# A gated unit turned and made from seven block products, with every engine's order laid out word by word

## The chip, the cores and the metric

One core of one Trainium2 chip runs the kernel. Its engines are TensorE (PE: matmuls, its weight loads shown as PEld), VectorE (DVE), ScalarE (ACT) and GpSimd (POOL); SyncE (SP) and POOL issue the transfers. The metric is the device time of one launch in microseconds, and the number to compare is the median of several runs. Inputs and outputs are float32 in the chip's memory. A matmul of full precision is made from halves: a float32 number is split into a high part, which the matmul form `fp32r` can hold, and a low part, and `high x high + high x low + low x high` makes three matmuls for one.

## The reference

With DEPTH = 1 there is one layer. Its mixer is the bidirectional S5 scan with a gated linear unit behind it, and its feed-forward part is a SwiGLU. There are 1024 tokens with 1024 features, 256 context tokens, and a hidden width of 2816 (22 tiles of 128). What matters here, shortened:

```python
def rms_norm(x, g):
    y = x * rsqrt(mean(x * x, -1, keepdims=True) + 1e-6)
    return y * g

# mixer, behind the scan that gives y (1024 tokens x 1024 features)
y = y + d_skip * h
g = gelu(y)
m = g * sigmoid(g @ w_glu + b_glu)          # the gated unit
x = x + gate0 * m                           # adaLN gate, residual
# feed-forward
h2 = rms_norm(x, norm_ffn) * (1 + scale1) + shift1
x = x + gate1 * ((silu(h2 @ w1) * (h2 @ w3)) @ w2)
return rms_norm(x, norm_final)
```

gate0, scale1, shift1 and gate1 are rows of 1024 features that the conditioning vector c gives.

## The kernel before

The kernel is one program with an order written by hand. Memory on the chip is cut into fixed regions (`r0`, `ra`, `ru`, `c0` to `c3`, `rxa`, `rxc`, `rw`), and code places views in them; PSUM comes from pools. The framework sets a wait wherever a buffer's last use isn't done, and each engine runs its own instructions in the order in which the code issued them.

The scan's part is driven by two strings of words, `PROG1` and `PROG2`, which `run()` carries out one after the other: a letter for the operation and a number for its index. In the trace the scan's recurrence on DVE ends at about 229 us. `PROG2` then finishes the scan's outputs block by block (k is a block of 128 features, of 8): words N, Q, Z and D make and add up the parts of block k, H applies GELU to it (ACT, from PSUM into the array `Y`, 128 partitions holding 128 token groups, 8 feature blocks x 8 token sets s x 128), I turns four of its 128x128 squares by transposes (`gt_hi`, L1056) and makes the high half, J the low half, w, l, W and V load and split weights, x multiplies Y by gate0 on POOL, and g starts the first matmuls.

The gated unit is then made with the activations as the stationary side. For token set s (128 tokens) and column quarter cq (256 outputs), `glu_unit(cq, s)` issues 8 x 3 matmuls of 128x256 (`glu_mm`, L1097 to L1099), adds the bias row on DVE (L77), applies the sigmoid on ACT (L1127), multiplies by gated g and adds x on DVE, and squares with a sum for the norm on ACT (L1134). There are 32 such units; first 16 for the first half of the tokens, then 16 for the second half. Between them generators run: `rms_steps` (L1157) makes the norm's factor on DVE, `h2s_steps` scales rows of Y on POOL, and `h2t_steps` transposes them back (L1177), applies scale and shift on ACT (L1186) or DVE (L86), and splits them (L1188 and L77). So `GH[0]` and `GH[1]` hold h2, turned, for the two token halves.

The first two FFN tiles follow plainly: `up_plain(ft, n)` makes 4 x 12 matmuls of 128x512 (`mm4` and `mm3`, L1286 to L1288) for token half n. `load2(0)`, behind `up_plain(0, 0)`, gates the first tile of w2 (`gate2`, 128x1024 on DVE) and splits it (cast on ACT, low half on POOL). The other twenty tiles are done two by two from seven products of blocks (`seq`, `produce`), which the change leaves as they are.

Names that recur: `tt` is a two-input elementwise instruction, and all its calls carry the helper's line L77 (L78 after the change), whatever engine they run on; `stt` is L80, `ts` L84 or L86. `split` makes both halves: a cast (ACT, by `S.copy`) and the subtraction of it (POOL or DVE). `MB` is a gate spread over the partitions, `mcol` the modulation rows as columns, `ident` the identity for transposes. In the profile's names, `pe`, `pu`, `pd`, `ut`, `xt`, `pt` are PSUM, and the rest are regions or small tiles (`r`).

Of the kernel before, what the change touches and what calls it, by code (L numbers as in the profile page):

```python
# [10 lines left out]
F32 = mybir.dt.float32  # L11
# [6 lines left out]
P = 128  # L18
# [13 lines left out]
PROG1 = ("A22 B0 A26 C02 G1 A30 A34 C03 A40 K0 A44 A48 C10 K1 L2 A54 G2 C11 A60 F10 C12 F11 C13 T0 T1 T2 T3 A64 M0 M1 K2 R0 P0 Y0 Y1 K3 L3 R1 C20 P1 Y2 Y3 T4 T5 G3 T6 T7 C21 C22 C23 K4 R2 P2 Y4 Y5 K5 R3 P3 Y6 Y7 T8 T9 T10 T11 C30 C31 R4 P4 Y8 Y9 C32 C33 R5 P5 Y10 Y11 M2 m0 F30 F31")  # L32
PROG2 = ("k6 Z0 N0 Z1 Z2 D0 Z3 N1 k7 D1 Z4 H0 H1 K6 N2 D2 H2 K7 T12 T13 T14 T15 N3 Z5 D3 H3 N4 D4 z6 z7 I0 J0 I1 J1 w0 w1 l1 H4 N5 D5 I2 J2 H5 I3 J3 W0 W1 x0 x1 x2 x3"
         " Q6 H6 I4 J4 Q7 b0 I5 J5 H7 g03 g13 I6 J6 g23 g05 g15 I7 J7 V1 w20 w21 g26 x10 x11 x12 x13")
# [8 lines left out]
def s5_ffn_kernel(tc, a, out):  # L43
# [3 lines left out]
    with ctx:  # L47
# [17 lines left out]
        RA = region("ra", 80.5)  # L65
# [3 lines left out]
        RW = region("rw", 6)  # L69

# [33 lines left out]
        modb = small([6, T])[:, 0:2]  # L104
# [49 lines left out]
        xr = a["x"].rearrange("(c s) d -> c s d", s=T)  # L154
# [799 lines left out]
        def run(prog):  # L954


            for w in prog.split():
# [40 lines left out]
                elif op == "N":  # L998
                    late[i] = [pe8([4, T, HC]) for _ in range(2)]
                    states_mm(i, late[i], 1, HSl[i], True)  # L1000
                elif op == "D":
                    for gp, po in enumerate(late[i]):
                        tt(yview(i, gp), po, yview(i, gp), ADD)
                elif op == "H":
                    if i in late:
                        S.activation(Y[:, i], Y[:, i], AF.Gelu_apprx_tanh)
                    else:
                        for gp in range(2):
                            S.activation(yview(i, gp), inner[i][gp], AF.Gelu_apprx_tanh)
                elif op == "I":  # L1010
                    if GH[0] is None:
                        GH[0] = tuple(view(region(t, 16, R32), 0, [4, 8, P]) for t in ("c1", "c0"))
                    late[i] = gt_hi(i, 0)
                elif op == "J":
                    gt_lo(i, 0, late[i])
                elif op == "W":
                    if not WR:
                        W0.append(region("c2", 16, R32))
                        WR.append((view(W0[0], 0, [8 * 256]), view(W0[0], 8, [8 * 256])))
                    v = slice(1024 * i, 1024 * i + 1024)  # L1020
                    split(wr0[i], (WR[0][0][:, v], WR[0][1][:, v]), E, V)
                elif op == "w":
                    cq, h = divmod(i, 10)
                    SY.dma_start(wr0[h], a["w_glu"][cq][:, 1024 * h:1024 * h + 1024])
                elif op == "b":
                    SY.dma_start(bglu, a["b_glu"].to_broadcast([P, D]))
                elif op == "l":
                    load_glu(i)
                elif op == "m":
                    mod_row(0)  # L1030
                elif op == "x":
                    gate(i % 10, slice(4 * (i // 10), 4 * (i // 10) + 4))
                elif op == "V":
                    GR.append(region("ra", 80.5, R32))
                    GH[1] = (view(GR[0], 0, [4, 8, P]), view(GR[0], 16, [4, 8, P]))
                    WR.extend((view(GR[0], kb, [8 * 256]), view(GR[0], kb + 8, [8 * 256])) for kb in (32, 48, 64))
                    split(wraw, WR[i], E)
                elif op == "g":
                    glu_mm(0, i // 10, range(i % 10 + 1))

        KT = {}
        late, W0, WR, PZ, GH, GR = {}, [], [], {}, [None, None], []
        wr0 = [view(RXa, 4, [1024]), view(RW, 0, [1024])]
        bglu = view(RU, 32, [D])
        wraw = view(RXc, 0, [2048])

        def load_glu(cq):
            SY.dma_start(wraw, a["w_glu"][cq])
# [4 lines left out]
        def gt_hi(k, half, eng=S):  # L1053
            pt = pe8([4, P])
            for i in range(4):
                PE.transpose(pt[:, i], Y[:, k, 4 * half + i], ident)  # L1056
            if eng is S:
                S.copy(GH[half][0][:, :, k], pt)
            else:
                eng.tensor_copy(GH[half][0][:, :, k], pt)  # L1060
            return pt

        def gt_lo(k, half, pt):
            h_, l_ = GH[half]
            tt(l_[:, :, k], pt, h_[:, :, k].bitcast(F32), SUB)

        def gt(k, half):
            gt_lo(k, half, gt_hi(k, half))

# [8 lines left out]
        def gh_(s):  # L1078
            h_, l_ = GH[s // 4]
            return h_[:, s % 4], l_[:, s % 4]  # L1080

        def gate(s, ks):
            y = Y[:, ks, s]
            n = y.shape[2] if len(y.shape) == 4 else 0
            g = MB.rearrange("p (k n) -> p k n", n=P)[:, ks]
            tt(y, y, bc(g, 2, n) if n else g, MUL, E)

        def glu_mm(cq, s, ks):

            wH, wL = (w.rearrange("p (k n) -> p k n", k=8) for w in WR[cq])  # L1090
            h_, l_ = gh_(s)
            new = (cq, s) not in PZ
            if new:
                PZ[cq, s] = [pe8([256]), 0]
            pz, n = PZ[cq, s]
            for k in ks[n:]:
                PE.matmul(pz, h_[:, k], wH[:, k], start=n == 0, stop=False)  # L1097
                PE.matmul(pz, h_[:, k], wL[:, k], start=False, stop=False)
                PE.matmul(pz, l_[:, k], wH[:, k], start=False, stop=n == 7)  # L1099
                n += 1  # L1100
            PZ[cq, s][1] = n
            return pz

# [7 lines left out]
        W0, GR = W0[0], GR[0]  # L1111
        X1 = region("c3", 16)
        xs = [view(X1, 4 * i, [D]) for i in range(4)]
        for s in range(4):
            SY.dma_start(xs[s], xr[:, s])
        TT = [[view(GR, 32 + 16 * i + 8 * j, [4, 4, P]) for j in range(2)] for i in range(3)]
        def glu_unit(cq, s, *others):

            def step():
                for g in others:  # L1120
                    next(g, None)

# [650 lines left out]
```

## Time and profile before

| what | us |
|---|---|
| runs shown | 1021.4, 1022.26, 1024.85 |
| median of them | 1022.26 |
| the profiled execution itself | 1024.33 |
| its span, first to last instruction | 1022.5 |
| mean clock granted to TensorE (share of full) | 0.987 |

All rows of the profile are of that one execution, 2.07 us above the median. In a row of a timeline stand start, duration, engine, line and operation, output and inputs (`out<-in`), shapes and count, and in brackets the idle time ahead of it with what ended it. In a row of groups stand the count behind the x, then busy time, the mean duration in nanoseconds, and the engine's idle time ahead of such instructions. Matmuls are pipelined, so that durations of neighbours overlap.

The chain of work that ended last is followed back by the profile to about 1000 us only, over DVE and ACT, which make the last norm and the outputs. The change doesn't touch that part, so the time ahead of it is read from PE's rows.

### The profile page before, as it was taken

Reading aid. Unit: us, or ns where it says so; the run is one execution under the profiler, and the core shown is the slowest. Engines: PE = TensorE matmul, PEld = TensorE weight load, DVE = VectorE, ACT = ScalarE, POOL = GpSimd, SP = SyncE. Lnnn points to the kernel's source line nnn. Section 1 sums busy time; section 2 is a strip of 40 time slices with the busy share of each in tenths; the row PEclk is TensorE's granted clock in tenths of the full one; section 3 lists DMA queues with packets and bytes.
Section 4 is the critical chain, followed back from the end, with each engine's and each line's share of the span. In section 5 each row is a group of like instructions: output and inputs, shape, how many; then the busy total and the mean of one; then the engine's idle time right before and its main releaser. Section 6 shows DMA issues by size and latency. Waiting matters only on the chain. (4 is left out here: it accounts for less than half of the span.)

```text
span 1022.5 us, 18552 instructions
## 1 busy us (share of the span) xinstructions
PE 962.6 (94%) x6988; PEld 774.2 (76%) x6988; DVE 785.6 (77%) x1642; ACT 438.5 (43%) x858; POOL 762.7 (75%) x590
## 2 busy tenths in 40 slices
PE   5987798868999999999999999999999999999996
PEld 1466523658999988778888888888888888888885
DVE  7989799994365778788968768585958778686977
ACT  5477622324353663533334343424333343324337
POOL 5799999991591457879686877778686877777664
PEclk9999999998999999999999999999999999999998
DMA  9765997222622021011212011121212111121205
GB/s 318 292 132 96 276 350 243 91 73 57 235 80 86 2 104 62 21 42 42 83 41 73 32 52 61 43 73 52 73 42 81 41 40 56 45 70 52 72 21 165
DMA packets 48546, 98.96 MB, mean 97 GB/s; under 512 B 4284, under 2 KB 18876, under 8 KB 47176
## 3 DMA queue, kind: packets, MB, share of 16 engines
q1 hardware_dynamic: 43272, 86.64, 25.3%
q0 software_dynamic: 2016, 7.34, 3.8%
q10 hardware_dynamic: 3168, 3.79, 1.1%
q8 instruction: 55, 0.90, 0.4%
q14 instruction: 35, 0.29, 0.1%
HBM read 84.25 MB, written 6.17 MB: 88 GB/s over the span
## 5 line engine op out<-in xcount | busy, mean ns | idle before, releaser
L77 POOL TENSOR_TENSOR c<-rxc,c 128x512 fp32r<-128x512 f32 x128 | 166.6, 1316 | 53.5 <-ACT c L1227 52.7
L1287 PE MATMUL ut<-ra,c 128*128 128x512 f32 x400 | 155.7, 389 | 1.2 <-DVE ra L77 1.2
L1286 PE MATMUL ut<-ra,c 128*128 128x512 f32 x400 | 155.7, 389 | 0.2 <-ACT ra L1227 0.2
L1288 PE MATMUL ut<-ra,c 128*128 128x512 f32 x400 | 155.6, 389 | 0.0
L1227 ACT CAST c<-rxc 128x512 fp32r<-128x512 f32 x128 | 79.1, 622 | 146.8 <-PE xt L1581 53.3
L1581 PE MATMUL xt<-c,c 128*128 128x512 f32 x540 | 129.7, 389 | 0.0
L1581 PEld LDWEIGHTS xt<-c,c 128*128 128x128 f32 x540 | 101.4, 188 | 21.0
L77 DVE TENSOR_TENSOR ru<-ru,xt 128x1024 f32<-128x1024 f32 x90 | 106.8, 1213 | 8.6 <-PE xt L1581 6.6
L77 DVE TENSOR_TENSOR ru<-ut,ru 128x512 f32<-128x512 f32 x98 | 67.1, 686 | 43.1 <-PE ut L1288 37.7
L1287 PEld LDWEIGHTS ut<-ra,c 128*128 128x128 f32 x400 | 75.1, 188 | 17.1 <-POOL rxc L77 1.5
L1286 PEld LDWEIGHTS ut<-ra,c 128*128 128x128 f32 x400 | 75.1, 188 | 16.1 <-ACT ra L1227 0.6
L1288 PEld LDWEIGHTS ut<-ra,c 128*128 128x128 f32 x400 | 75.1, 188 | 15.5
L77 POOL TENSOR_TENSOR c<-rw,c 128x512 fp32r<-128x512 f32 (+1 forms) x29 | 42.5, 1465 | 38.8 <-ACT c L1227 38.2
L1286 PE MATMUL ut<-c,c 128*128 128x512 f32 x160 | 62.3, 389 | 0.8 <-DVE rxa L77 0.8
L77 POOL TENSOR_TENSOR c<-ru,c 128x512 fp32r<-128x512 f32 (+1 forms) x39 | 55.5, 1422 | 10.1 <-ACT c L1227 5.7
L77 POOL TENSOR_TENSOR rxc<-rxc 128x512 f32<-128x512 f32 x40 | 61.5, 1536 | 1.6
L1288 PE MATMUL ut<-c,c 128*128 128x512 f32 x160 | 62.3, 389 | 0.0
L1287 PE MATMUL ut<-c,c 128*128 128x512 f32 x160 | 62.3, 389 | 0.0
L1581 PE MATMUL ut<-c,c 128*128 128x512 f32 x216 | 51.9, 389 | 0.0
L584 PE MATMUL pv<-ru,c 128*64 128x160 f32 x512 | 43.7, 312 | 7.3 <-POOL ru L77 2.6
L77 DVE TENSOR_TENSOR pe<-pe,ru 128x256 f32<-128x256 f32 x64 | 27.4, 428 | 29.5 <-ACT pe L1127 17.4
L77 DVE TENSOR_TENSOR ru<-ru,ut 128x512 f32<-128x512 f32 x76 | 47.2, 678 | 0.7 <-ACT ru L1635 0.5
(449 smaller groups left out, 2576.0 us busy)
## 6 DMA issues: line engine op xcount, KB each, us to landing
c<-in_ada_w SPq DMA_DIRECT2D x46, 256.0 KB
rxc<-in_w SPq DMA_DIRECT2D x38, 256.0 KB
rxc<-in_w SPq DMA_DIRECT2D x19, 512.0 KB
ru<-in_w SPq DMA_DIRECT2D x11, 512.0 KB
rw<-in_w SPq DMA_DIRECT2D x11, 512.0 KB
ra<-in_ada_w SPq DMA_DIRECT2D x10, 512.0 KB
ra<-in_ada_w SPq DMA_DIRECT2D x18, 256.0 KB
ru<-in_xT SPq DMA_DIRECT2D x4, 1024.0 KB
```

The source lines that it names most:

```text
L77: eng.tensor_tensor(out=o, in0=x, in1=y, op=op)
L584: PE.matmul(pv[64 * (i % 2):64 * (i % 2) + 64, ri, c0:c0 + 160], w[:, i, 64 * ri:64 * ri + 64], U[:, 8 * b + 4 * j + i], start=True, stop= ...
L1227: S.copy(o[0], x)
L1286: PE.matmul(pu, wh, bh, start=start, stop=False)
L1287: PE.matmul(pu, wh, bl, start=False, stop=False)
L1288: PE.matmul(pu, wl, bh, start=False, stop=stop)
L1581: PE.matmul(pd, w[:, cs_], b, start=j in (1, 2, 4) and n == 0, stop=n == 2, skip_group_check=j not in (1, 2, 4))
```

## The change

The gated unit is turned. The weights are now stationary (128x128), the activations moving (512 tokens), and output features lie on the partitions. Weights and activations are cut into 2x2 blocks of 512, and the four output blocks come from seven products of sums of blocks instead of eight products. Product p for a column block q of 128 features takes 4 x 3 matmuls of 128x512 (L1218). `ORDER` names the sides; the second product adds up in the banks of the first.

- Weight sums contain only plus signs, and are made by transfers that add to what lies at their destination: `wadd` and the words a and h add a block from the chip's memory, s and f add one buffer to another. All eight are issued by POOL. Minus signs have gone into the sums of activations, which DVE makes (words m, t2, t3, t4). Blocks of weights are loaded six times (w, l, c, and the adding a and h) instead of four.
- GELU is applied behind the turn (`gelu_turn`, gA), from PSUM into `YT`, the turned g; H is a plain copy now.
- Outputs add up in PSUM and in Y's space (words p, u, v, c, d1, d2, E1, all 128x512). Then come a sigmoid with the bias as a column (eS), one instruction that multiplies by gate0's column and g (eM), and the addition of x (eX), which is loaded turned (`a["xt"]`, a layout made on the host). The gate on POOL and the spread-out gate0 row are gone.
- The result is turned back for the residual (bT, bC: 16 turns of four transposes), and its squares are summed by token (q; bQ and bR).
- The norm's factors (z) are spread along the tokens by four fp32 matmuls with the identity for each half (Z: `rows`, L1150). h2 then comes without transposes: hT scales, hH or hI and hC shift and cast, hL makes the low half.
- Region `ra` is handed back behind the scan and cut into five buffers (`rr0` to `rr4`). PSUM there has five banks for products (`pp`), two for turns (`pq`) and one for the rows (`prb`).
- The string `TODO` sets the order of all of it, for every engine: each word issues one operation, a dot or a number issues one or more steps of PE, three matmuls each. There are 128 steps: 112 of products, and 16 for `up_plain(0, 0)`, whose matmuls (`mm3`, now L1356 to L1358) now belong to the string; `up_plain(0, 1)` follows it. A last letter names an engine: A is ACT, D or V is DVE, P or E is POOL.
- The first tile of w2 is gated and split inside the string (L:g at step 84, L:h and L:l at steps 111 and 113) instead of behind `up_plain(0, 0)`, and its load (Q) is issued earlier.

The core of the diff:

```diff
-PROG2 = ("k6 Z0 N0 Z1 Z2 D0 Z3 N1 k7 D1 Z4 H0 H1 K6 N2 D2 H2 K7 T12 T13 T14 T15 N3 Z5 D3 H3 N4 D4 z6 z7 I0 J0 I1 J1 w0 w1 l1 H4 N5 D5 I2 J2 H5 I3 J3 W0 W1 x0 x1 x2 x3"
-         " Q6 H6 I4 J4 Q7 b0 I5 J5 H7 g03 g13 I6 J6 g23 g05 g15 I7 J7 V1 w20 w21 g26 x10 x11 x12 x13")
+PROG2 = ("k6 Z0 N0 Z1 Z2 D0 Z3 N1 k7 D1 Z4 K6 N2 D2 K7 w0 T12 T13 T14 T15 w1 l0 l1 c0 N3 Z5 D3 N4 D4 z6 z7 I0 J0 I1 J1 N5 D5 I2 J2 I3 J3 W0 a0 W1 a1"
+         " Q6 H6 I4 Q7 b0 c1 I5 H7")
...
                 elif op == "H":
-                    if i in late:
-                        S.activation(Y[:, i], Y[:, i], AF.Gelu_apprx_tanh)
-                    else:
-                        for gp in range(2):
-                            S.activation(yview(i, gp), inner[i][gp], AF.Gelu_apprx_tanh)
+                    for gp in range(2):
+                        S.copy(yview(i, gp), inner[i][gp])
...
+        def wload(w, h, m, i):
+            SY.dma_start(w[h], wpart(h, m, i))
+
+        def wadd(w, h, m, i):
+            E.dma_start(w[h], wpart(h, m, i), accum_op=ADD)
...
+        def gelu_turn(k, j, pool=pe8):
+            pt = pool([4, P])
+            four(pt, lambda i: Y[:, k, 4 * j + i])
+            S.activation(YT[j][:, k], pt.rearrange("p s c -> p (s c)"), AF.Gelu_apprx_tanh)
...
-                PE.matmul(pz, h_[:, k], wH[:, k], start=n == 0, stop=False)
-                PE.matmul(pz, h_[:, k], wL[:, k], start=False, stop=False)
-                PE.matmul(pz, l_[:, k], wH[:, k], start=False, stop=n == 7)
...
+        def rows(j, pool):
+            RBC[j] = pool([4, P])
             for i in range(4):
+                PE.matmul(RBC[j][:, i], rb[:, i], ident, start=True, stop=True)
...
+        ORDER = (("L11", "R11"), ("L12", "R21"), ("S2", "T2"), ("S3", "T3"), ("L22", "T4"), ("S1", "T1"), ("S4", "R22"))
+        TODO = """gT:6:0 x:0 . Wh:L12:1 . Rh:R21:0 Wl:L12:1 gT:7:0 Rh:R21:1 . gA:6:0 . gA:7:0 Wh:L12:0 gT:1:1 Rl:R21:0:D s:0 gT:4:1 . Rh:R21:3
...
+            bR:2:1 bT:3:1 hL:0:7:E bC:3:1:A bQ:3:1 bR:3:1 . z:1 . S:0 3 Z:1 . hT:1:0 . hT:1:2 hH:1:0 . hT:1:1 hH:1:2 . hL:1:0:V hI:1:1 hL:1:2:V
...
+            cs_, z = slice(P * q, P * q + P), ZT[4 * p + q]
+            for n, (w, b) in enumerate(((lh, rh), (lh, rl), (ll, rh))):
+                PE.matmul(z, w[:, k, cs_], b[:, k], start=p != 1 and k + n == 0, stop=k == 3 and n == 2, skip_group_check=p == 1)
...
+            elif op in ("s", "f"):
+                o, x = (wc, wa) if op == "s" else (wb, wc)
+                E.dma_start(o[n], x[n], accum_op=ADD)
+            elif op == "m":
+                tt(A1[n], YT[1][:, n], YT[0][:, n], SUB)
+            elif op == "t2":
+                tt(A2[:, n], YT[1][:, 4 + n], A1[n], SUB)
...
+                if op == "eS":
+                    S.activation(z, z, AF.Sigmoid, bias=bgc[:, k:k + 1])
+                elif op == "eM":
+                    stt(y if v[-1] == "s" else z, z, mcol[:, 0, k:k + 1], y, MUL, MUL)
+                else:
+                    tt(y, y if eng is E else z, x[:, v[1]], ADD, eng)
...
+                if op == "hT":
+                    stt(t, YT[j][:, k], mod2[:, 1, k:k + 1], flat4(RBC[j]), MUL, MUL)
...
+                elif eng is V:
+                    stt(l_, t, f, h_.bitcast(F32), ADD, SUB)
...
+        for word in TODO.split():
+            todo(word)
...
-        up_plain(0, 0, rest, {2: lambda: together(h2t_steps(7, pf, tba[1], 0), h2t_steps(7, pf, tba[1], 1))})
-        load2(0)
```

Where instructions stand on three engines, before and now (a row is a line, an operation, output and inputs, and how often it comes in a run).

On PE in the old gated unit, at its start: matmuls of the first units in groups of three (`c_3191` is a weight half, `c_3120` and `c_3121` are halves of g), among them the turns of blocks 6 and 7 (L1056).

```order
L1056 MATMUL pe<-r_60,ru 128x128 x4
L1097 MATMUL pe<-c_3191,c_3120 128x256
L1098 MATMUL pe<-c_3191,c_3120 128x256
L1099 MATMUL pe<-c_3191,c_3121 128x256
L1097 MATMUL pe<-c_3191,c_3120 128x256
L1098 MATMUL pe<-c_3191,c_3120 128x256
L1099 MATMUL pe<-c_3191,c_3121 128x256
L1056 MATMUL pe<-r_60,ru 128x128 x4
```

And now, at the start of the first product (`pq` are turns, `pp` the product's banks):

```order
L1062 MATMUL pe<-r_60,ru 128x128 x4
L1246 MATMUL pq<-r_60,ru 128x128 x4
L1218 MATMUL pp<-c_3123,c_3192 128x512 x6
L1246 MATMUL pq<-r_60,ru 128x128 x4
L1218 MATMUL pp<-c_3123,c_3192 128x512 x6
L1246 MATMUL pq<-r_60,ru 128x128 x8
L1218 MATMUL pp<-c_3123,c_3192 128x512 x9
L1246 MATMUL pq<-r_60,ru 128x128 x8
L1218 MATMUL pp<-c_3123,c_3192 128x512 x12
L1246 MATMUL pq<-r_60,ru 128x128 x8
L1218 MATMUL pp<-c_3123,c_3192 128x512 x9
L1246 MATMUL pq<-r_60,ru 128x128 x8
```

The turns of the second token half have moved from among the units to the first product, where two banks take them.

On POOL, from the end of the scan's work on; before: low halves of weights (`c_3191`, `ra`) and gates of Y (`ru<-ru,rxa`).

```order
L77 TENSOR_TENSOR c_3191<-rxa,c_3191 128x1024
L77 TENSOR_TENSOR c_3191<-rw,c_3191 128x1024
L77 TENSOR_TENSOR ru<-ru,rxa 128x4x128 x4
L77 TENSOR_TENSOR ra<-rxc,ra 128x2048
L77 TENSOR_TENSOR ru<-ru,rxa 128x4x128 x4
L77 TENSOR_TENSOR ru<-ru,rxa 128x2x512
L77 TENSOR_TENSOR ra<-rxa,ra 128x1024
L77 TENSOR_TENSOR ra<-rw,ra 128x1024
L77 TENSOR_TENSOR ru<-ru,rxa 128x2x512 x2
L77 TENSOR_TENSOR ra<-rxc,ra 128x2048
```

Now: low halves of weights (`c_3192`, `rr_3376`, `rr_3378`) and of activations (`rr_3377`), and between them the adding transfers that POOL issues (L1049 from memory, L1277 from buffer to buffer).

```order
L78 TENSOR_TENSOR c_3192<-rxa,c_3192 128x1024
L1049 DMA rxa<-in_w_glu 128x1024
L78 TENSOR_TENSOR c_3192<-rw,c_3192 128x1024
L1049 DMA rw<-in_w_glu 128x1024
L78 TENSOR_TENSOR rr_3376<-rxc,rr_3376 128x1024
L1277 DMA rxa<-rxa 128x1024
L78 TENSOR_TENSOR rr_3376<-rxc,rr_3376 128x1024
L1277 DMA ru<-rw 128x1024
L78 TENSOR_TENSOR rr_3377<-c_3122,rr_3377 128x512
L1277 DMA rxc<-rxa 128x1024
L78 TENSOR_TENSOR rr_3378<-rxa,rr_3378 128x1024
L1277 DMA rxc<-ru 128x1024
```

The gates are gone, and each adding transfer stands behind the low half that read its destination.

On DVE at the end of the stage; before: bias and product of the last unit (L77), scale and shift of rows turned by `h2t_steps` (L86), then the last norm factor.

```order
L86 TENSOR_SCALAR pe<-pe,r_60 128x128 x4
L77 TENSOR_TENSOR pe<-pe,ru 128x256
L77 TENSOR_TENSOR ru<-pe,c_3450 128x2x128
L77 TENSOR_TENSOR ra<-pe,ra 128x512
L1157 TENSOR_REDUCE r_60<-r_60 128x1
L86 TENSOR_SCALAR r_60<-r_60 128x1 x2
L84 TENSOR_SCALAR r_60<-r_60 128x1
L77 TENSOR_TENSOR r_60<-r_60 128x1
L80 SCALAR_TENSOR_TENSOR r_60<-r_60 128x1 x2
L77 TENSOR_TENSOR r_60<-r_60 128x1
L80 SCALAR_TENSOR_TENSOR r_60<-r_60 128x1 x2
L77 TENSOR_TENSOR r_60<-r_60 128x1
```

Now, ahead of the second half's norm (L1141): output blocks' ends (`pp<-pp,ru`, `pp<-pp,r_60,rr_3375`, `rr_3375<-pp,c_3373`), low halves (`rr_3377<-rxa,r_60,rr_3376`), scaled rows (`rxa<-c_3122,r_60,prb`) and sums of squares (L1252).

```order
L81 SCALAR_TENSOR_TENSOR rxa<-c_3122,r_60,prb 128x512
L78 TENSOR_TENSOR rr_3375<-pp,c_3373 128x512
L78 TENSOR_TENSOR pp<-pp,ru 128x512
L81 SCALAR_TENSOR_TENSOR rr_3377<-rxa,r_60,rr_3376 128x512
L1252 TENSOR_REDUCE r_60<-ru 128x4
L81 SCALAR_TENSOR_TENSOR rxa<-c_3122,r_60,prb 128x512
L81 SCALAR_TENSOR_TENSOR pp<-pp,r_60,rr_3375 128x512
L1252 TENSOR_REDUCE r_60<-ru 128x4
L78 TENSOR_TENSOR rr_3375<-pp,c_3373 128x512
L1252 TENSOR_REDUCE r_60<-ru 128x4 x2
L1141 TENSOR_REDUCE r_60<-r_60 128x4
```

And behind that norm, from the copy that feeds the row matmuls (L1143) on:

```order
L1143 COPY rw<-r_60 128x512
L81 SCALAR_TENSOR_TENSOR r_60<-rr_3375,r_60,prb 128x512
L81 SCALAR_TENSOR_TENSOR rxa<-rr_3375,r_60,prb 128x512 x2
L81 SCALAR_TENSOR_TENSOR c_3192<-r_60,rr_3378 128x512
L81 SCALAR_TENSOR_TENSOR c_3192<-rxa,r_60,rr_3378 128x512
L81 SCALAR_TENSOR_TENSOR r_60<-rr_3375,r_60,prb 128x512
L81 SCALAR_TENSOR_TENSOR rxa<-rr_3375,r_60,prb 128x512
L78 TENSOR_TENSOR ru<-pp,ru 128x512
L81 SCALAR_TENSOR_TENSOR c_3192<-r_60,rr_3378 128x512
L81 SCALAR_TENSOR_TENSOR rxa<-rr_3375,r_60,prb 128x512
L81 SCALAR_TENSOR_TENSOR r_60<-rr_3375,r_60,prb 128x512
L81 SCALAR_TENSOR_TENSOR c_3192<-rxa,r_60,rr_3378 128x512
```

The norm of the last tokens was a factor for one token set, with scaling and turning behind it; it is now one of four token sets, with the rows and the scaled operands of half the tokens behind it.

More of the change, by code (lines that the diff above doesn't have):

```diff
@@ new lines, in pr_, with prod, xload @@
+        def pr_(shape=(4, P)):
+            return pG.tile([P] + list(shape), F32, tag="r", name="prb", bufs=1)
+        def prod(pz, l, r, q, start):
+            (lh, ll), (rh, rl) = SL[l], SL[r]
+            cs_ = slice(P * q, P * q + P)
+            for k in range(4):
+                for n, (w, b) in enumerate(((lh, rh), (lh, rl), (ll, rh))):
+                    PE.matmul(pz, w[:, k, cs_], b[:, k], start=start and k + n == 0, stop=k == 3 and n == 2, skip_group_check=not start)
+        def xload(o, i, j):
+            SY.dma_start(o.rearrange("p k (s c) -> p k s c", s=4), a["xt"][:, 4 * i:4 * i + 4, 4 * j:4 * j + 4])
```

450 lines of the change are left out of this document (250 added, 200 removed).

## Prediction

> **What bounds the kernel now.** I read the page's busy shares first, then its forty slices, then a table of windows cut at the borders of the stages, and at last single matmuls.
>
> ```profile
> PE 962.6 (94%) x6988; PEld 774.2 (76%) x6988; DVE 785.6 (77%) x1642; ACT 438.5 (43%) x858; POOL 762.7 (75%) x590
> PE   5987798868999999999999999999999999999996
> PEclk9999999998999999999999999999999999999998
> ```
>
> TensorE (PE) is busy for 94% of the span, and solidly from the eleventh slice on; its clock is full there. The windows say where its idle time lies (columns: stretch, length, then busy time and count by engine, granted clock, DMA share, GB/s).
>
> ```profile
> core 0: us, PE busy (x) PEld busy (x) DVE busy (x) ACT busy (x) POOL busy (x), PEclk, DMA share, GB/s
> 229.00:267.70 38.70, 35.68 (x986) 33.21 (x984) 17.62 (x27) 14.23 (x21) 10.56 (x11) 0.92 0.41 125
> 267.70:381.90 114.20, 114.20 (x921) 112.25 (x920) 71.89 (x201) 64.54 (x168) 62.02 (x42) 1.00 0.25 84
> 381.90:460.00 78.10, 75.70 (x330) 61.52 (x329) 60.62 (x87) 32.66 (x58) 63.41 (x45) 1.00 0.12 41
> 460.00:1022.50 562.50, 553.95 (x2444) 458.34 (x2443) 429.10 (x504) 219.53 (x396) 424.97 (x315) 1.00 0.18 60
> ```
>
> The third row is the stage of the change: gated unit, second norm, and the first half of the first FFN tile's up products. In its 114.20 us PE never rests, while DVE, ACT and POOL have 42 to 52 us each to spare. So work taken from PE comes off the end, until one of the three becomes the bound.
>
> **What leaves PE.** Single matmuls of the stage (start, duration, engine and line):
>
> ```profile
> 288.65 0.28 PE L1097 MATMUL pe<-ra,c 128*128 128x256 f32 x1
> ...
> 291.05 0.28 PE L1099 MATMUL pe<-ra,c 128*128 128x256 f32 x1
> 291.17 0.60 PE L1056 MATMUL pe<-r,ru 128*128 128x128 f32 x4
> 291.52 0.36 PE L1097 MATMUL pe<-ra,c 128*128 128x256 f32 x1
> ```
>
> Durations overlap in the pipeline, so a price is the distance of starts: from 288.65 to 291.05 there are 20 steps, 0.120 us each. The old gated unit has 32 units x 8 x 3 = 768 of them: **92.2 us**. Four transposes (a turn) take 0.35 us, and the first matmul behind them 0.08 more.
>
> **What comes to PE.** Seven products x 4 column blocks x 4 x 3 = 336 matmuls of 512 columns, their stationary side changed each time. The first FFN tile is such a run already:
>
> ```profile
> 393.31 0.39 PE L1286 MATMUL pd<-c 128*128 128x512 f32 x1
> ...
> 404.21 0.39 PE L1286 MATMUL pd<-c,c 128*128 128x512 f32 x1
> ```
>
> 48 steps in 10.90 us are 0.2271 us each: 336 make **76.3 us**. The turns stay 26 in the stage (104 transposes): 10 of activations either way, then 16 back instead of 16 of the normalised rows. The check on the old stage: 92.2 + 48 x 0.2271 (10.9) leave 11.1 us for 26 turns, 0.43 each. New are eight fp32 matmuls that spread the norm's row over the partitions. The nearest row is the scan's, where sixteen records are eight such matmuls:
>
> ```profile
> 205.36 2.05 PE L945 MATMUL pw<-ra,ru 128*128 128x128 f32 x16
> ...
> 207.35 0.49 PE L922 MATMUL pw<-c,ra 64*64 64x128 f32 x4
> ```
>
> That is **2.0 us**. PE's work falls by 92.2 - 76.3 - 2.0 = **13.9 us**, the stage from 114.2 to 100.3 if nobody makes it wait. [...]
>
> **Who can make PE wait.** The other engines' work in the stage, counted in the table of words and priced by these rows:
>
> ```profile
> L77 POOL TENSOR_TENSOR c<-rxc,c 128x512 fp32r<-128x512 f32 x128 | 166.6, 1316 | 53.5 <-ACT c L1227 52.7 <-PE xt L1288 0.7
> L77 POOL TENSOR_TENSOR ra<-rxa,ra 128x1024 fp32r<-128x1024 f32 x1 | 2.4, 2398 | 0.0
> L433 POOL DMA_DIRECT2D c<-c x8: 861/866/878, 55.9 to 106.4; - x8
> L77 DVE TENSOR_TENSOR ru<-ru,ut 128x512 f32<-128x512 f32 x76 | 47.2, 678 | 0.7 <-ACT ru L1635 0.5
> L1227 ACT CAST c<-rxc 128x512 fp32r<-128x512 f32 x18 | 10.5, 616 | 6.2 <-POOL rxc L77 5.3 <-PE ut L1287 0.7 <-PE pu L1287 0.2
> L1073 ACT CAST c<-rw 128x1024 fp32r<-128x1024 f32 x1 | 1.0, 1043 | 0.0
> ```
>
> By the last step POOL has 25 adds of 512 and 13 of 1024, 25 x 1.32 + 13 x 2.40 = 64 us, and six DMA issues of 0.87, 5 us. DVE has about 100 operations of 0.68 us, a 1024-wide gate and two norm chains, 76 us. ACT has 13 operations of 1024 and about 104 of 0.62 us, 78 us. Each alone fits under 100 us. But two do not run side by side freely:
>
> ```profile
> 503.38 1.29 POOL L77 TENSOR_TENSOR c<-rxc,c 128x512 fp32r<-128x512 f32 x1 [1.43 <-ACT c L1227]
> 503.44 1.78 DVE L77 TENSOR_TENSOR c<-rxa,c 128x512 fp32r<-128x512 f32 x1
> ...
> L77 DVE TENSOR_TENSOR c<-r,c 128x512 fp32r<-128x512 f32 x18 | 25.6, 1423 | 0.0
> L77 DVE TENSOR_TENSOR r<-r,rxa 128x512 f32<-128x512 f32 x9 | 6.1, 681 | 0.0
> ```
>
> DVE's low half from two SBUF inputs starts 0.06 us after POOL's add and ends 0.56 us after it: 1.78 us, its wait included. Without POOL alongside the same shape takes 0.68, and with an input from PSUM (`ru<-ru,ut`, above) too. So I add POOL's adds to DVE's two-SBUF operations as if they were one engine. In the first 64 of the table's 128 steps (three matmuls each) that sum is 8 x 1.32 + 9 x 2.40 + 28 x 0.68 = 51.2 us, while PE needs 64 x 0.681 + 12 turns x 0.43 = 48.7. By step 128 it is 35 DVE operations, a 1024-wide gate and POOL's 64, some 89 us against 100.3. The table runs POOL and DVE level with PE in its first half and has room in its second. [...]
>
> **Waits, bounded from both sides.**
> - *Ahead.* In 229.0 to 267.7 a plain copy of 0.6 us on ACT stands where GELU stood, the POOL gates of Y are gone, and weight loads are issued earlier on SP's queue and added to on POOL's. PE idles 38.70 - 35.68 = 3.0 us there, mostly for scan work that stays. A third of that could go, or come: -1 to +1, and I take 0.
> - *Start.* The first turns have two PSUM banks, and ACT empties them by GELU, between weight casts: about 7.6 us of ACT in the first eight steps, against 8 x 0.681 + 6 x 0.43 = 8.0 of PE. Behind a late GELU, PE's queue holds the product's matmuls. Nothing, to 2 us (three ACT operations); I take 0.7, the one that trails.
> - *Middle.* A weight sum goes DMA issue on POOL, landing, ACT's cast, POOL's low half, in front of 12 to 24 matmuls. Landing is covered by a product or more of 10.9 us each:
>
> ```profile
> c<-c POOLq DMA_DIRECT2D x8, 512.0 KB, 5.3
> ```
>
>  Uncovered, what counts is the shared access: 51.2 - 48.7 = 2.5 us, with the six issues (5 us) in POOL's own queue. 0 to 6; I take 2, near the plain excess. The four loads of turned x on SP's queue are issued twenty steps or more before use; at the stage's 84 GB/s 1 MB lands in 12.5 us, a product later, so they cost nothing.
> - *End.* The second half's norm needs the last output. DVE's chain between the two norm rows is 34 operations and the norm itself:
>
> ```profile
> 1001.31 0.60 DVE ru L77
> 1001.98 0.60 DVE ru L77
> ...
> 321.37 0.16 DVE L1157 TENSOR_REDUCE r<-r 128x4 f32<-128x16 f32 x1
> ...
> 323.56 0.36 DVE L80 SCALAR_TENSOR_TENSOR r<-r 128x4 f32<-128x4 f32 x2
> ```
>
>  At the chain's pace of 0.60, with 2.6 us for the norm and 0.6 for a copy: 34 x 0.60 + 3.2 = 23.6 us. PE meanwhile has 28 steps, 7 turns and four row matmuls: 19.1 + 3.0 + 1.0 = 23.1. They end together. Behind the rows PE has four steps (2.7 us) until the second half's operands are wanted, and the fourth of those is DVE's ninth operation (5.4 to 6.1 us), wanted at about 4.8. Nothing, if DVE runs ahead; 7 us, if the four two-SBUF operations in the chain and five behind it each lose 0.74 us (9 x 0.74 = 6.7). I take 3, less than half.
> - *After.* The first down tile is gated and split inside the stage: 1.2 to 2.2 us of DVE, 1.0 of ACT, 2.4 of POOL fewer behind it, with its load earlier on SP's queue.
>
> ```profile
> 426.92 0.47 PE L1286 MATMUL ut<-c,c 128*128 128x512 f32 x1 [0.78 <-DVE rxa L77]
> ...
> 456.29 0.47 PE L1287 MATMUL ut<-ra,c 128*128 128x512 f32 x1 [1.25 <-DVE ra L77]
> ```
>
>  PE waited for DVE twice there. At best the longer wait goes (-1.2), at worst moved buffers make another such (+1.5); I take 0.
>
> Sum: -13.9 + 0 + 0.7 + 2 + 3 + 0 = **-8.2 us**. The profiled execution took 1024.33 us (span 1022.5, and 1.8 around it), so it would be 1016.1. The median of the runs is 2.07 lower: 1022.26 - 8.2 = **1014.1 us**. With every term at its least it is 1022.26 - 16.1 = 1006.2, with every one at its most 1022.26 - 13.9 + 17.5 = 1025.9.
>
> **Rivals.**
> A. *No waits*: the table's cover holds, 1022.26 - 13.9 = **1008.4**. For it: each engine fits alone. Against: the first half's sum lies above PE's time.
> C. *Waits of 9 to 13 us*: end and middle near their upper bounds, **1017.4 to 1021.4**. For it: PE has only two turn banks and four steps of cover at the end.
> D. *Slower: the shared access becomes the bound.* Each of DVE's 42 two-SBUF operations (seven stand behind the last step) loses 1.42 - 0.68 = 0.74 us to POOL, 31 us in all. It decides once over 13.9 us of this stands in PE's way, 19 of the 42. With two thirds, -13.9 + 20.7 gives **1029**. For it: the row of 1.78 us. Against: DVE is free for 24 us and POOL for 31 of the 100.
> E. *It doesn't save what it says*: if the 512-column form ran at 0.26 us here, for its changing weights, 336 x 0.033 = 11 us would go, and **1019.5** remain even without waits. Against: the FFN's rows.
>
> **How the numbers follow.** About 0.3% (3.07 us) is what a measurement of this kernel can tell from no change, so "same" is 1019.2 to 1025.3. A has 0.20, the forecast (waits of 2 to 9 us, 1010.4 to 1017.4) 0.52, C 0.18 of which 0.10 is "same", D 0.07, E 0.03. Faster is 0.20 + 0.52 + 0.08 = 0.80, same 0.10 + 0.03 = 0.13, slower 0.07. The range leaves out A's lower half (0.10), D (0.07) and C's last end (0.02): 1008.8 to 1021.
>
> **What would show it.** PE should show 336 matmuls 0.227 us apart where 768 were, and idle time of about 6 us between the scan's end and the second half's up products: short waits for ACT at the first turns, for POOL or DVE in the first half, and the longest for DVE around the second norm. DVE's two-SBUF operations should average 0.9 to 1.4 us. I am wrong if waits at one of these places pass its bound, if the matmuls' distance isn't 0.227, or if the FFN behind moves by over 1.5 us.

## The result, and the profile after

The changed kernel takes 1031.2 us (median of 4 runs, 1030.57 to 1031.87), the kernel before 1023.55 us (1021.4 to 1025.14; a fourth run has come to the three shown ahead): **0.76% slower**, ratio 1.0076 with the interval [1.0052, 1.0100]. The prediction was 1014.1 us, faster, with a range of 1008.8 to 1021. The profiled execution took 1031.7 us (span 1029.9), 7.4 more than the one before.

The same rows of the page as before:

```profile
PE 957.5 (93%) x6572; PEld 750.8 (73%) x6572; DVE 820.9 (80%) x1580; ACT 450.3 (44%) x827; POOL 773.7 (75%) x595
PE   5988798878998798999999999999999999999996
PEclk9989999989999899999999999999999999999998
```

PE has less work, yet the tenths show holes in three slices where there were none (the 13th, 14th and 16th), and the clock line dips in one of them, the 14th. The windows, cut at the same places in the program (the gated unit's first turns, the second token half's first up product, a later point of the FFN):

```profile
core 0: us, PE busy (x) PEld busy (x) DVE busy (x) ACT busy (x) POOL busy (x), PEclk, DMA share, GB/s
229.00:267.40 38.40, 34.35 (x985) 32.10 (x986) 15.70 (x27) 11.09 (x19) 12.55 (x13) 0.96 0.51 143
267.40:390.40 123.00, 106.28 (x507) 86.74 (x504) 106.76 (x136) 78.65 (x137) 73.22 (x45) 0.96 0.38 102
390.40:468.30 77.90, 77.65 (x335) 63.75 (x336) 64.28 (x91) 33.62 (x60) 61.53 (x44) 0.98 0.12 41
468.30:1029.90 561.60, 553.13 (x2438) 457.07 (x2436) 428.29 (x504) 219.83 (x397) 425.11 (x315) 1.00 0.19 60
```

All of it is in the second row. The stage took 114.4 us from its first matmul (267.5 to 381.9), and now takes 123.0. What is before it and behind it is the same or 1.1 us shorter. PE is idle for 123.0 - 106.3 = 16.7 us of it, where it was idle for none, and its mean granted clock fell from 1.00 to 0.96. DVE is busy for 106.8 us where its operations counted to 76. PE's waits, from its timeline (the idle time and what ended it stand in brackets):

```profile
269.17 0.50 PE L1218 MATMUL pp<-c,c 128*128 128x512 f32 x1 [1.22 <-ACT ru L1007]
297.47 1.05 PE L1218 MATMUL pp<-rr,rr 128*128 128x512 f32 x2 [1.87 <-DVE rr L78]
338.33 0.47 PE L1246 MATMUL pq<-r,c 128*128 128x128 f32 x1 [6.50 <-DVE c L78]
356.87 0.60 PE L1150 MATMUL prb<-r,rw 128*128 128x128 f32 x3 [2.28 <-DVE rw L1143]
378.06 0.41 PE L1246 MATMUL pq<-r,rr 128*128 128x128 f32 x2 [0.86 <-ACT ru L1250]
379.85 0.50 PE L1357 MATMUL pp<-rr,rr 128*128 128x512 f32 x1 [0.85 <-POOL rr L78]
383.64 0.38 PE L1150 MATMUL prb<-r,rw 128*128 128x128 f32 x1 [0.33 <-DVE rw L1143]
390.37 0.76 PE L1356 MATMUL pu<-rr,rr 128*128 128x512 f32 x1 [2.82 <-ACT rxa L1324]
```

These eight make the 16.7 us. The longest is for DVE, in the middle. In its last part and behind it the clock was halved, as these windows show:

```profile
336.00:338.30 2.30, 0.00 (x0) 0.00 (x0) 2.27 (x4) 0.29 (x1) 2.01 (x2) 0.50 0.94 296
340.00:342.00 2.00, 2.00 (x7) 1.61 (x6) 1.06 (x2) 1.63 (x5) 0.00 (x0) 0.50 0.00 0
344.00:346.00 2.00, 2.00 (x12) 1.65 (x11) 1.94 (x3) 1.72 (x5) 0.00 (x0) 1.00 0.00 0
```

And this is what DVE did ahead of that wait, with POOL's timeline beside it:

```profile
317.73 2.12 DVE L78 TENSOR_TENSOR rr<-c,rr 128x512 fp32r<-128x512 f32 x1
319.77 8.55 DVE L78 TENSOR_TENSOR rr<-ru,rr 128x512 fp32r<-128x512 f32 x1
328.25 1.27 DVE L78 TENSOR_TENSOR ru<-ru,pp 128x512 f32<-128x512 f32 x2
```

```profile
319.59 0.89 POOL L1049 DMA_DIRECT2D ru<-in_w_glu  x1 [0.30 <-POOL rr L78]
320.21 2.73 POOL L78 TENSOR_TENSOR rr<-rxa,rr 128x1024 fp32r<-128x1024 f32 x1
322.58 1.60 POOL L78 TENSOR_TENSOR c<-rr,c 128x512 fp32r<-128x512 f32 x1
323.83 2.69 POOL L78 TENSOR_TENSOR c<-rxc,c 128x1024 fp32r<-128x1024 f32 x1
326.18 1.58 POOL L78 TENSOR_TENSOR c<-rr,c 128x512 fp32r<-128x512 f32 x1
329.55 2.81 POOL L78 TENSOR_TENSOR rr<-ru,rr 128x1024 fp32r<-128x1024 f32 x1 [1.79 <-ACT rr L1261]
```

One low half of 0.68 us lasted 8.55 us. It came up while POOL issued an adding transfer, waited through the four adds that stood behind it in POOL's queue, and ended 0.56 us after the last of them (327.76), where POOL had to wait for ACT. Before it, at 317.73, a like operation had waited for one POOL add only (2.12 us). Two more operations lasted 4.58 us (287.78) and 4.94 us (304.18), each behind a transfer issued by POOL.

### The profile page after: what moved, and what is told of

It reads as the page before. It is cut to its first block, busy times and chain, and to the rows that moved or that the text cites. A ratio compares the mean times of both kernels' runs of the same rounds, so it can differ in the third digit from the quotient of the medians.

```text
span 1029.9 us, 17603 instructions
## 1 busy us (share of the span) xinstructions
PE 957.5 (93%) x6572; PEld 750.8 (73%) x6572; DVE 820.9 (80%) x1580; ACT 450.3 (44%) x827; POOL 773.7 (75%) x595
## 5 line engine op out<-in xcount | busy, mean ns | idle before, releaser
L78 POOL TENSOR_TENSOR rr<-rxc,rr 128x512 fp32r<-128x512 f32 (+1 forms) x130 | 172.6, 1341 | 63.1 <-ACT rr L1187 56.2
L1358 PE MATMUL ut<-rr,rr 128*128 128x512 f32 x400 | 155.7, 389 | 0.2 <-POOL rr L78 0.2
L1356 PE MATMUL ut<-rr,rr 128*128 128x512 f32 x400 | 155.6, 389 | 0.0
L1187 ACT CAST rr<-rxc 128x512 fp32r<-128x512 f32 x124 | 76.9, 622 | 148.3 <-PE xt L1680 51.5
L1680 PE MATMUL xt<-rr,c 128*128 128x512 f32 x540 | 129.7, 389 | 0.0
L1357 PE MATMUL ut<-c,rr 128*128 128x512 f32 x320 | 124.5, 389 | 0.0
L1680 PEld LDWEIGHTS xt<-rr,c 128*128 128x128 f32 x540 | 101.4, 188 | 21.0
L1357 PE MATMUL ut<-rr,rr 128*128 128x512 f32 x240 | 93.4, 389 | 0.0
L1358 PEld LDWEIGHTS ut<-rr,rr 128*128 128x128 f32 x400 | 75.1, 188 | 16.3 <-POOL rr L78 0.6
L1356 PEld LDWEIGHTS ut<-rr,rr 128*128 128x128 f32 x400 | 75.1, 188 | 15.6
L1357 PEld LDWEIGHTS ut<-c,rr 128*128 128x128 f32 x320 | 60.1, 188 | 12.4
L78 POOL TENSOR_TENSOR rr<-ru,rr 128x512 fp32r<-128x512 f32 (+1 forms) x40 | 58.7, 1468 | 9.5 <-ACT rr L1187 5.7
L1356 PE MATMUL ut<-c,rr 128*128 128x512 f32 x160 | 62.3, 389 | 0.1
L1358 PE MATMUL ut<-c,rr 128*128 128x512 f32 x160 | 62.2, 389 | 0.0
L1680 PE MATMUL ut<-rr,c 128*128 128x512 f32 x216 | 51.9, 389 | 0.0
L1357 PEld LDWEIGHTS ut<-rr,rr 128*128 128x128 f32 x240 | 45.0, 188 | 9.3
L1218 PE MATMUL pp<-rr,rr 128*128 128x512 f32 x192 | 48.1, 407 | 1.9 <-DVE rr L78 1.9
```

What stands on the lines that cost most here:

```text
L78: eng.tensor_tensor(out=o, in0=x, in1=y, op=op)
L1187: S.copy(o[0], x)
L1218: PE.matmul(z, w[:, k, cs_], b[:, k], start=p != 1 and k + n == 0, stop=k == 3 and n == 2, skip_group_check=p == 1)
L1356: PE.matmul(pu, wh, bh, start=start, stop=False)
L1357: PE.matmul(pu, wh, bl, start=False, stop=False)
L1358: PE.matmul(pu, wl, bh, start=False, stop=stop)
```

## The experiments

**Theory 1**: behind a transfer that POOL issues, DVE's two-SBUF operations get no turn until POOL's queue runs dry. **Theory 2**: the two take turns as predicted, and there is simply too much for them. **Theory 3**: DVE waits for the transfer itself.

**m_lock.** A small kernel that does nothing but such operations, in stretches with and without a transfer:

```diff
+        for kind, n, width, nr, nv, fence in SECTIONS:
...
+            E.tensor_tensor(out=pc[:, 0:512], in0=go, in1=pb[:, 0:512], op=OP.add)
+            if kind == "add":
+                E.dma_start(w, a["w_glu"][1, 0][:, 0:1024], accum_op=OP.add)
...
+            for i in range(nv):
+                V.tensor_tensor(out=vc, in0=va, in1=vb, op=OP.add)
...
+            for i in range(n):
+                E.tensor_tensor(out=pc[:, 0:width], in0=pa[:, 0:width], in1=pb[:, 0:width], op=OP.add)
```

> A kernel that leaves out the whole computation and only copies the turned x out. In 13 stretches POOL runs 4 or 6 adds of two SBUF inputs back to back, with or without an issue of a 512 KB transfer ahead of them, and DVE comes in with three adds of two SBUF inputs (0.68 us each when free) about when the transfer is issued. Theory 1 (behind a transfer issued by POOL, DVE's two-SBUF operations get no turn until POOL's queue runs dry): without a transfer DVE's first add takes at most one POOL add and itself, 2.0 us beside 512-wide and 3.1 beside 1024-wide adds; behind the issue it takes the whole burst, 6 x 1.3 + 0.6 = 8 us and 4 x 2.4 + 0.6 = 10 us, with 1 or 2 adds of 1024 in the burst 3 and 5.4, and with a POOL instruction behind the issue that waits for DVE's first add it is at most 1.5. Theory 2 (POOL and DVE simply take turns, the stage has too much work for both): the same 2.0 and 3.1 us with and without the transfer. Theory 3 (DVE waits for the transfer's own data): about 5 to 8 us behind every transfer, even where POOL has no adds.

Neither 8 nor 10 us was seen. The first waiting add took 1.63 us beside 512-wide adds and 2.71 us beside 1024-wide ones without a transfer, 2.20 and 3.14 us with an adding one, and with a transfer but no adds on POOL 0.7. That refutes theory 3, and theory 1 in this form. But these POOL adds all wrote one buffer, so that each waited for the one before it; in the stage they don't. **m_lock2** gives each its own buffer:

```diff
-                E.tensor_tensor(out=pc[:, 0:width], in0=pa[:, 0:width], in1=pb[:, 0:width], op=OP.add)
+                o = pd[i] if own else pc
+                E.tensor_tensor(out=o[:, 0:width], in0=pa[:, 0:width], in1=pb[:, 0:width], op=OP.add)
```

> The small kernel again (the whole computation left out), now with an output buffer of its own for each POOL add, so that no add waits for the one before it; in the first small kernel all adds wrote one buffer, and DVE was let in after each of them, with or without a transfer. Theory 1a (a transfer issued by POOL, then adds that don't wait for one another): without a transfer DVE's second add takes at most 2 us beside 512-wide and 3.1 us beside 1024-wide adds; behind the issue 6 x 1.3 + 0.6 = 8 us and 4 x 2.4 + 0.6 = 10 us; with one shared output 2.2 as before. Theory 1b (adds that don't wait for one another are enough): 8 and 10 us with and without the transfer. If neither shows, at most 3.2 us everywhere, something else in the stage holds DVE off.

DVE's first waiting add, from the timeline of m_lock2: without a transfer (26.85), behind an adding one (40.43), behind a plain one (54.80), with one shared output (83.11), and coming 2 us after the issue ended (174.78):

```profile
26.85 1.63 DVE L86 TENSOR_TENSOR vc<-va,vb 128x512 f32<-128x512 f32 x1
...
40.43 8.27 DVE L86 TENSOR_TENSOR vc<-va,vb 128x512 f32<-128x512 f32 x1
...
54.80 7.86 DVE L86 TENSOR_TENSOR vc<-va,vb 128x512 f32<-128x512 f32 x1
...
83.11 2.07 DVE L86 TENSOR_TENSOR vc<-va,vb 128x512 f32<-128x512 f32 x1
...
174.78 5.88 DVE L86 TENSOR_TENSOR vc<-va,vb 128x512 f32<-128x512 f32 x1
```

```profile
39.76 1.01 POOL L78 DMA_DIRECT2D w<-in_w_glu  x1
40.50 7.63 POOL L89 TENSOR_TENSOR pd<-pa,pb 128x512 f32<-128x512 f32 x6
48.20 0.54 POOL L91 COPY go<-pd 128x4 f32<-128x4 f32 x1
```

Theory 1a holds: 8.27 us behind a transfer, 1.63 without. In these runs it took both, a transfer issued by POOL and adds behind it that wait for nothing: with one shared output, where each add waits for the one before it, DVE's add took 2.07 us behind the transfer. It made little difference whether the transfer adds (7.86 us behind the plain one). Beside four 1024-wide adds it was 10.01 us. Without a transfer DVE's add waited for one of POOL's (26.22 to 27.93) and ended 0.55 us after it; behind one it waited for all six (40.50 to 48.13) and ended 0.57 us after the last.

In the kernel itself the transfers were taken from POOL (**a_nodma**), kept there without the addition (**a_plain**), or followed by a stop of POOL's queue (**a_fence**):

```diff
# a_nodma
-            E.dma_start(w[h], wpart(h, m, i), accum_op=ADD)
+            SY.dma_start(w[h], wpart(h, m, i))
...
-                E.dma_start(o[n], x[n], accum_op=ADD)
+                SY.dma_start(o[n], x[n])
# a_plain
-            E.dma_start(w[h], wpart(h, m, i), accum_op=ADD)
+            E.dma_start(w[h], wpart(h, m, i))
...
-                E.dma_start(o[n], x[n], accum_op=ADD)
+                E.dma_start(o[n], x[n])
# a_fence
+            elif op == "F":
+                E.tensor_copy(junk1[:, 0, 0:1], (A3[v[1]] if n == "A3" else SL[n][1][:, v[1]].bitcast(F32))[:, 0:1])
...
-t3:2 . Rl:T2:3:P
+t3:2 F:A3:2 . Rl:T2:3:P
...
-h:0 . Rl:T3:3:D .
+h:0 . Rl:T3:3:D F:T3:3 .
...
-h:1 . Rl:T1:3:D Rh:R22:0
+h:1 . Rl:T1:3:D F:T1:3 Rh:R22:0
```

> The changed kernel with the eight adding transfers of the gated unit issued by SP as plain transfers of the same size; the weight sums are left out. Theory 1: DVE's two-SBUF operations in the stage stay below 3.3 us (8.55 in the changed kernel), PE's idle 6.5 us ahead of the turn at 338 us falls below 2, the slow clock behind it goes too, and the time comes to 1018 to 1024 us against 1031.2. Theory 2: POOL saves 6 x 0.87 = 5 us of its own, of which PE sees at most 3: 1028 or more.

> The changed kernel with the eight transfers still issued by POOL, but without the addition; the weight sums are left out. If the issue by POOL does it, the time is as the changed kernel's within 2 us (1029 to 1033) and DVE's longest two-SBUF operation stays above 6 us. If the addition does it, as without POOL's transfers: 1018 to 1024.

> The changed kernel with three one-column copies added on POOL, each behind one of the last three transfers it issues ahead of a burst, reading what DVE's next two-SBUF operation writes, so that POOL's queue stops there until DVE is through. Theory 1: DVE's three long operations (4.6, 4.9 and 8.6 us) fall below 2.2, the wait at 338 us below 3, time 1020 to 1026 us. Theory 2: POOL loses up to 1 us at each, the time is the same or up to 3 us longer.

| kernel | median us | against the kernel before, same chip | longest two-SBUF DVE operation, us |
|---|---|---|---|
| a_nodma | 1024.81 | 1.0001 [0.9983, 1.0020] | 2.89 |
| a_plain | 1035.76 | 1.0109 [1.0072, 1.0147] | 14.09 |
| a_fence | 1020.42 | 0.9963 [0.9945, 0.9981] | 2.88 |

Three one-column copies turn 0.76% slower into 0.37% faster, some 11 us (1031.2 to 1020.4): the waits at 297 and 338 us are gone altogether, DVE's three long operations take 0.68, 0.68 and 0.69 us, and the time lies where theory 1 had it. The third copy stands where the 8.55 us were:

```profile
316.68 0.18 POOL L1279 COPY ru<-rr 128x1 f32<-128x1 f32 x1 [1.41 <-DVE rr L78]
316.83 2.40 POOL L78 TENSOR_TENSOR rr<-rxa,rr 128x1024 fp32r<-128x1024 f32 x1
```

a_nodma came out 0.8 us above its range. Turn by turn without a stop, DVE is still late enough for a wait of 2.53 us at that place, and the transfers stand in another queue. a_plain was expected within 2 us of the changed kernel and came 4.6 us above it (0.33% or 3.4 us by the ratios, whose intervals overlap): its adds found no wait for seven instructions, and the same low half lasted 14.09 us. So the issue does it, not the addition, and the length of POOL's unbroken run sets the price: 8.55 us behind four adds, 14.09 behind seven instructions.

**a_fence1** keeps only the third copy.

> The changed kernel with only the last of the three small POOL copies, behind the transfer at 319.6 us in front of the 8.55 us operation. Theory 1: of the 10.8 us that all three brought, the wait of 6.5 us at 338 us and its slow clock (about 1.5 us) go, the wait of 1.9 us at 297 us stays: 1021.5 to 1025.

It took 1026.33 us, 1.0027 [1.0009, 1.0044], 1.3 us above the range. The wait at 297 us stayed (1.90), but a wait of 1.86 us remained at the turn where it had been 6.50: with the two earlier operations still long, DVE comes late there too. By the ratios the last copy brings 0.49% (5.0 us) and the first two 0.64% (6.5 us).

**f_z0** works on a_fence: two splits of up weights go behind the first norm.

```diff
-z:0 eS:d:1 2 oh:0:0 . oh:0:2 ol:0:0 d1:2 bT:4:1 oh:0:3 Z:0 eM:d:1:s bC:4:1:A
-            ol:0:2 d2:2 oh:0:1 .
+z:0 eS:d:1 2 . d1:2 bT:4:1 Z:0 eM:d:1:s bC:4:1:A oh:0:0 oh:0:2 ol:0:0 oh:0:3
+            ol:0:2 d2:2 oh:0:1 .
```

> The kernel with the three small POOL copies, and two splits of the first up weights moved behind the first half's norm, so that POOL has no add beside it. Theory: the wait of 2.28 us ahead of the first row matmuls comes from two operations of the norm (128x4, 0.16 us each) that POOL's adds held for 1.13 and 1.19 us; the wait falls by about 2 us to below 0.5, with the slow clock behind it (1.6 us): 2 to 3.6 us off the stage's end up to the next wait, in the time 1 to 3.5 us. Rival: the chain is late anyway, 1 us or less.

In the changed kernel the norm's tiny operations wait for POOL's adds, as the large ones do (DVE, then POOL):

```profile
353.80 1.13 DVE L78 TENSOR_TENSOR r<-r 128x4 f32<-128x4 f32 x1
354.97 1.39 DVE L81 SCALAR_TENSOR_TENSOR r<-r 128x4 f32<-128x4 f32 x2
```

```profile
353.61 2.53 POOL L78 TENSOR_TENSOR rr<-rxc,rr 128x512 fp32r<-128x512 f32 x2 [1.46 <-ACT rr L1266]
```

With the splits moved the two rows take 0.17 and 0.36 us, the wait falls from 2.28 to 0.30, and from the first product to the second half's up products PE takes 108.3 us (270.97 to 379.26) where a_fence took 111.5 (269.26 to 380.80). The time is 1017.32, 0.9951 [0.9936, 0.9966]: 3.1 us under a_fence by the medians, 1.2 by the ratios, since the two ran on two chips; the intervals overlap, so the gain in time is not fixed closer than that. Nor is it all the wait: of the 3.2 us in the stage, PE's waits make 0.6 (4.0 us in a_fence, 3.4 here). The rest goes with the granted clock, which was 0.50 twice for 3.4 us in a_fence's stretch (from 345.7 and 369.6) and 1.00 throughout in this one.

**f_bank** and **f_m0** ask what ends the wait of 2.82 us at the second half's first up product. f_bank (on a_fence) hands out that pool's banks in another order, f_m0 (on f_z0) moves a word:

```diff
# f_bank
         FIRST[:] = [pt_(), pt_()]
+        pu_()
# f_m0
-hL:1:0:V hI:1:1 hL:1:2:V
-            hC:1:1 hT:1:3 hL:1:1:E hT:1:5 hH:1:3 M:0 hI:1:5
+hL:1:0:V hI:1:1 M:0 hL:1:2:V
+            hC:1:1 hT:1:3 hL:1:1:E hT:1:5 hH:1:3 hI:1:5
```

> The kernel with the three small POOL copies, and the next PSUM pool's two up banks handed out in the other order, so that the first matmul of the second token half no longer takes the bank that DVE reads last (word M:0). Theory: the wait of 2.81 us there is for that bank; it falls to about 1 us, the slow clock behind it (six matmuls of 0.43 us) goes, and the time falls by 1.5 to 3 us against the kernel with the copies (1020.4): 1017.4 to 1018.9. Rival: the wait is for h2's halves from ACT, as the profile names it, and the time stays within 1 us.

> The kernel with the three small POOL copies and the moved splits (1017.3), and DVE's product M:0 put three operations earlier, behind the first low half of the second token half. The other order of banks left PE's first matmul of that half waiting for M:0 all the same. If M:0 ends the wait of 2.84 us there, PE starts three DVE operations (2.0 us) earlier and waits about 0.8 us, and the later halves then cost up to 1 us: time 1 to 2.5 us lower, 1014.8 to 1016.3. If ACT's scaled rows end it, as the profile names it, no change within 0.5 us.

f_bank changed nothing: 1020.80, 0.9981 [0.9966, 0.9996], the same wait (2.83), where 1017.4 to 1018.9 was expected. Its rival, ACT, is wrong all the same: with M:0 earlier the wait falls to 0.87 (and 0.55 one block later), and in f_z0 as in f_m0 PE starts 0.15 us behind the end of M:0 (at 379.26 and 376.12). The profile's releaser there was the event that came last by its account, not the one that PE needed. Yet the time stayed, 1017.93, 0.9949 [0.9935, 0.9962], above the 1014.8 to 1016.3 expected. PE now waits 1.27 us at the first down product, for DVE, nearly what was won:

```profile
393.77 0.50 PE L1358 MATMUL pd<-c 128*128 128x512 f32 x1 [1.27 <-DVE ru L78]
```

**f_w2late** (on a_fence) undoes the early gating of the first down weights.

```diff
-bT:4:0 L:g x:3
+bT:4:0 x:3
...
-eX:E:1:D L:h .
+eX:E:1:D .
-eM:E:2 L:l .
+eM:E:2 .
...
+        load2(0)
         up_plain(0, 1, rest)
```

> The kernel with the three small POOL copies, and the first tile of w2 gated and split between the first and the second token half's up products, as before the change. If gating early helps, the time rises by 1 to 3 us, with a wait at the first down products; if its cast, add and gate are in the way around the second norm, PE's two waits of 0.86 us there shrink and the time falls by 0.5 to 2 us; I expect no more than 1 us either way.

1024.10, 1.0010 [0.9996, 1.0023], where a_fence had 0.9963: 0.47% or 4.8 us more. The first down products wait for DVE,

```profile
397.48 0.50 PE L1358 MATMUL pd<-c 128*128 128x512 f32 x1 [2.03 <-DVE ru L78]
```

and the waits of 0.86 us around the second norm stay. Behind that wait the granted clock was 0.50 for 3.4 us (from 398.8). So this part of the change helps, by more than the 1 us I gave it.

**f_h7** (on f_m0) makes the last block of h2 on ACT and DVE:

```diff
-eM:E:3 hI:0:7 bR:1:1
+eM:E:3 bR:1:1
-bQ:2:1 hC:0:7
+bQ:2:1 hH:0:7
-hL:0:7:E
+hL:0:7:V
```

> The kernel with M:0 moved, and the last block of the first half's h2 made by one ACT operation and a low half on DVE instead of two ACT operations and a low half on POOL. ACT loses 0.6 us and POOL 1.3 us in the stretch where PE waits 1.06 us for ACT and 0.84 us for that low half; DVE gains 0.74 us, and the second norm behind it is as much later. I expect 0 to 1 us less than with M:0 moved alone; if DVE's chain to the norm sets the end, 0 to 0.7 us more.

1016.64, 0.9941 [0.9926, 0.9955]. The wait of 0.85 for POOL is gone, and 0.46 of it comes back ahead of the norm's rows; the stage is as long as f_m0's (106.28 us from the first product in both), so the 1.3 us between the medians are not shown to come from this edit. **This version beats both kernels**: 0.6% under the one before, 1.3% under the changed one.

## Why the prediction was wrong

- *What leaves and comes to PE: right in kind, some 2.5 us too good.* 336 matmuls stand 0.227 us apart. f_h7 shows the whole sum: its stage takes 108.1 us (265.9 to 374.0) with 5.1 us of waits above 0.3, so 103.0 without, against 100.3. The other 2.7 us are spread over turns, the first matmuls behind them and shorter waits; no run takes them apart. Rival E is out.
- *Start: 0.7 forecast, 1.2 measured.* In bounds.
- *Middle: this step failed.* It gave 2 us (0 to 6); the waits of 1.87 and 6.50 us make 8.4, and the halved clock about 3.6 more (half of 3.4 us from 297.7, and half of the 3.8 us that PE worked at it from 338.3). The working added POOL's adds and DVE's two-SBUF operations "as if they were one engine" that serves them in turn. Six issues of transfers were priced at 0.87 us each in POOL's queue, and nothing else. What the runs showed in its place: behind such an issue one DVE operation lasted until 0.56 us after POOL's run of adds had ended, 4.6, 4.9 and 8.6 us in all. The trace before could not show it: from 48 to 142 us, where its fourteen transfers from POOL stand, every two-input operation of DVE has an input in PSUM.
- *End: 3 forecast (0 to 7), 7.1 measured* (2.28 + 0.86 + 0.85 + 0.33 + 2.82), just past its bound. The mechanism of half of it was in the text, DVE's chain around the norm; its size was off. The chain was priced at 0.60 us an operation and ran at 0.66 (`SCALAR_TENSOR_TENSOR` rows); the norm's small operations were taken as free of POOL's adds, and weren't; and M:0 was not seen as a wait.
- *After: 0 forecast, -1.1 measured.* In bounds, and f_w2late shows that the early gating is what keeps it there.
- *The clock: not in the sum.* Mean 0.96 in the stage; it cost the 3.6 us named above. Together the stage is -13.9 + 16.7 of waits + 3.6 of clock + 2.2 for the rest of PE's work = 8.6 us longer, and with the 1.2 saved beside it the span is 7.4 longer.
- Rival D named the shared access, the direction and the sum: 31 us lost by DVE. Measured are 30 us in the stage (1.5 us an operation, where 0.9 to 1.4 was named). But it spread them evenly, 0.74 us on each of 42 operations; 22 of the stage's 37 stayed at 0.7 to 0.8 us, and three took 16 of the 30 us. In a_nodma, where none takes over 2.89 us, DVE still loses 25 us, and of the two middle waits one is left, at 2.53 us: that speaks for the lumps having done the greater part of the harm, though taking turns isn't free either. In a_fence the loss itself falls to 16 us. The 7% given to D was too little.

With the three lumps, the held norm and M:0 out of the way, the time lies in the range after all: f_h7's 1016.6 us, 0.59% or 6.0 us under the kernel before on its own chip (4.6 to 7.6 by the interval), where 8.2 were forecast. That is another kernel than the one predicted, and its stage has no halved clock.

## What to carry to other kernels

Where POOL issues transfers and DVE has operations with two SBUF inputs beside it, look at what stands in POOL's queue behind each issue: put a wait there (a one-column copy of DVE's result; three of them took some 11 us off the changed kernel). An add that needs that result, or the issue at the end of POOL's run, was not tried here. A busy sum per engine tells whether a stage can fit; who is held for how long must be read from single instructions, the smallest ones of a dependency chain too. And a wait of PE can cost more than its length: around three of the four longest in the changed kernel (6.50, 2.82 and 1.87 us) the granted clock was 0.50, for 6.8, 3.4 and 3.4 us.

## What was not expected of the hardware

- Behind an adding transfer issued by POOL, adds of 512 that wait for nothing started 1.22 us apart in m_lock2, each recorded as starting some 0.33 us before the one ahead ended, and DVE's two-SBUF operation waited for all of them: 8.27 us for six, and in a_plain, where the transfer doesn't add, 14.09 for seven of mixed width. Without the transfer the two took turns (1.63 us).
- The granted clock fell to 0.50 behind some pauses (matmuls 0.427 us apart instead of 0.227) and not behind others of like length. In the changed kernel it did around the waits of 1.87, 6.50 and 2.82 us, for 3.4, 6.8 and 3.4 us from 297.7, 335.3 and 389.9, but not behind the one of 2.28 us at 356.87:

```profile
297.70:301.10 3.40, 3.40 (x11) 2.67 (x11) 3.37 (x6) 1.97 (x3) 3.40 (x3) 0.50 0.00 1
354.00:360.00 6.00, 3.72 (x23) 3.09 (x22) 5.90 (x10) 2.96 (x5) 3.98 (x4) 1.00 0.00 0
```

In a_fence it did behind 2.28 us and behind two pauses of 0.86 us within 2 us, but not behind 2.81 us; in f_z0 not behind 2.84 us. What decides between like pauses is not shown: no run here was made to test it.

- A two-SBUF DVE operation of 128x4 lasted 1.13 us beside POOL's adds (353.80 in the changed kernel), and 0.17 us in f_z0, where the splits stand behind the norm.
